# QKV of layer 0 in four K-chunks fed by chunks of modulation products, and four output-projection units in step with attention

## The chip, the cores and the metric

The kernel runs on one NeuronCore of one Trainium2 chip. The metric is the device time of one execution in microseconds (us). Five engines work beside each other, each through its own instructions in order: TensorE (PE: matmuls; PEld: its weight loads), VectorE (DVE), ScalarE (ACT), GpSimd (POOL) and SyncE (SP, which here only issues DMAs). They wait for one another by semaphores.

## The reference

A decoder trunk of two layers on 256 tokens with model width 2048. Each layer is a mixer and a squared-ReLU MLP, both behind an RMS norm with shift and scale from a conditioning vector c, and with a gate on the way back into x. Cut to what the change touches:

```python
cond = silu(c)
for i in range(2):
    mod = cond @ mod_w[i] + mod_b[i]                 # 2048 x (6*2048)
    sh1, sc1, g1, sh2, sc2, g2 = split(mod, 6)
    h = rms_norm(x, norm_mix[i]) * (1 + sc1) + sh1
    y = swa_sink_attention(h, ...) if i == 0 else hgrn2_mixer(h, ...)
    x = x + g1 * y
    h = rms_norm(x, norm_mlp[i]) * (1 + sc2) + sh2
    x = x + g2 * (relu(h @ w1) ** 2 @ w2)

def swa_sink_attention(h, w_in, w_out, q_gain, k_gain, sinks):
    q, k, v = split(h @ w_in, [2048, 2304])          # 32 query heads, 4 kv heads of 64
    q, k = rms_norm(q) * q_gain, rms_norm(k) * k_gain
    # banded blocks of 128 queries against 256 keys, ALiBi, softmax with a sink per head
    return softmax_with_sink(q @ k.T ...) @ v @ w_out
```

All is float32. The change is in layer 0 alone: the modulation products that its norms need, QKV, attention, the output projection and the first quarter of its MLP.

## The kernel before, in words

**Layout.** Activations lie transposed, 16 K-blocks of 128 partitions by 256 tokens. Weights are cut into items of 128 x 2048 floats (1 MB). One table, `seq`, lists all the items of the kernel in one order: weight items ("w") and modulation items. `put` builds it: it lays a stage's weights down and lets modulation items in between them, as its `per` function says. SP issues the loads in this order into five raw buffers (`NRAW`), so a load starts when the item five places ahead of it has been consumed.

**A weight item** (`prep_one`, L237 and L238) is split in two halves: ACT casts a half to a rounded high part `wh`, DVE subtracts to get the low part `wl`. There are buffers for five halves of each (`NW`). A product of float32 accuracy is then three matmuls for each K-block (`three`): wh with the high part of the activation, wh with the low part, wl with the high part. A unit of 128 output columns over 16 K-blocks is 48 matmuls of 256 columns; a weight item always carries 48.

**A modulation item** comes in two kinds. Kind "m" is one column block of 128 outputs: DVE multiplies the transposed weights with the broadcast `cond` and sums (L226, one instruction over 2048 elements and one that reads the accumulator). Kind "g" is a quarter of the K range for four column blocks: PE multiplies four groups of 512 columns in float32 with c as a 32-column weight (`gemv`); four such items make a set, and then ACT copies the row out of PSUM, PE turns it with four transposes (`gt`), and DVE reduces it into `mods`.

**The order of layer 0.** First 16 "m" items (shift and scale 1 of K-blocks 0 to 7), of which `make_h` makes h of the first eight K-blocks. Then QKV: ten items over K-blocks 0 to 7 (`mm_half`), with eight "m" items between them; five over K-blocks 8 to 11 (`mm_quarter`), with eight "m" items; five over K-blocks 12 to 15. The sums of the K-ranges are kept in `parts`: ACT copies the first, DVE adds the second (`add_part`, L798), and the last goes on to the head norms (`done_part`). Behind the last quarter come 24 "g" and four "m" items (gate 1, and scale and shift 2 of the first blocks).

Attention runs in 21 steps (`step`), three after each of the last three QKV items. Step s makes the scores of head pair s (`pair`), turns the probabilities of pair s-3 (`pair_t`), multiplies pair s-4 with v (`pair_v`), and takes up to two modulation items (`GPS`). Once 16 steps are done, two output-projection units start (`mm_std` with `count=2`), and the remaining steps run between their K-blocks. Then `open_mlp` runs the other 14 output units mixed with eight items of the first MLP quarter over K-blocks 0 to 7 (`order`: "o" and "u"), with one modulation item before each, and eight items over K-blocks 8 to 15 ("h", `mm_half`). Each "o" unit ends in a residual update (L568), in `make_u` for the first eight blocks (L553) and in a norm sum (L486). After that come the rest of MLP 0 and layer 1.

**What sets the order of an engine.** The program is written as one list of calls, and a scheduler with a cost model of its own fixes each engine's order before the run. `hook` and `later` place small follow-up work a few slots on. On the chip no engine passes over a waiting instruction.

## Time and profile before

| what | value |
|---|---|
| median of 3 runs | 2331.94 us (2331.55 to 2334.79) |
| profiled execution, its own time | 2334.28 us |
| its span in the trace | 2332.5 us |
| granted TensorE clock, mean | 0.987 |
| PE busy | 2263.7 us, 97% of the span |
| DVE busy | 1818.7 us, 78% |
| ACT busy | 1166.8 us, 50% |
| DMA, mean over the span | 257 GB/s |

The busy share is an average over stages that differ. In the page's 40 slices PE shows "2" in the first and "9" or "8" in all others, so what PE does not use lies almost wholly in the first 60 us; layer 0 up to the end of the opening of its MLP is the first fifth of the span.

### The profile page before, as it was taken

Reading aid. Unit: us, or ns where it says so; the run is one execution under the profiler, and the core shown is the slowest. Engines: PE = TensorE matmul, PEld = TensorE weight load, DVE = VectorE, ACT = ScalarE, POOL = GpSimd, SP = SyncE. Lnnn points to the kernel's source line nnn. Section 1 sums busy time; section 2 is a strip of 40 time slices with the busy share of each in tenths; the row PEclk is TensorE's granted clock in tenths of the full one; section 3 lists DMA queues with packets and bytes.
Section 4 is the critical chain, followed back from the end, with each engine's and each line's share of the span. In section 5 each row is a group of like instructions: output and inputs, shape, how many; then the busy total and the mean of one; then the engine's idle time right before and its main releaser. Section 6 shows DMA issues by size and latency. Waiting matters only on the chain.

```text
span 2332.5 us, 36840 instructions
## 1 busy us (share of the span) xinstructions
PE 2263.7 (97%) x14538; PEld 1986.2 (85%) x14538; DVE 1818.7 (78%) x3061; ACT 1166.8 (50%) x1974; POOL 3.5 (0%) x10
## 2 busy tenths in 40 slices
PE   2989999999999999999999999999999999999999
PEld 0986489998888888888888988899888888888888
DVE  8888788966988988887998988767866766655665
ACT  2435754544444444455666666655544444444443
POOL 0000000000000000000000000000000000000000
PEclk6999999999999999999999999999999999999999
DMA  9987789556989889885577777545666666555552
GB/s 379 344 311 287 295 319 365 200 183 244 341 319 340 319 326 334 322 304 181 210 280 267 257 271 266 201 166 181 226 244 219 249 231 229 209 182 194 184 197 93
DMA packets 84637, 598.79 MB, mean 257 GB/s; under 512 B 9456, under 2 KB 11504, under 8 KB 12272
## 3 DMA queue, kind: packets, MB, share of 16 engines
q1 hardware_dynamic: 81936, 593.81, 70.7%
q8 instruction: 114, 1.87, 0.3%
q10 hardware_dynamic: 2304, 2.10, 0.3%
q0 software_dynamic: 224, 0.52, 0.1%
q14 instruction: 59, 0.48, 0.1%
HBM read 594.04 MB, written 2.10 MB: 256 GB/s over the span
## 4 chain that ended last, share of the span: by engine, by line
PE 94%; DVE 4%; DMA 1%; ACT 1%; issue 1%; ACTq 0%; DVEq 0%
PE mm L50 89%; DVE raw L226 2%; DVE wl L238 1%; PE S L50 1%; PE A L50 1%; PE pv L50 1%; PE pt L50 1%; DMA raw<-in_mod_w_dram 1%; PE on L50 0%; PE cb L50 0%; ACT wh L237 0%; PE ss L50 0%; DVE ht L534 0%; PE ssq L50 0%; PE sst L50 0%
## 5 line engine op out<-in xcount | busy, mean ns | idle before, releaser
L237 ACT CAST wh<-raw 128x1024 fp32r<-128x1024 f32 x744 | 779.3, 1051 | 892.3 <-PE mm L50 801.8
L238 DVE TENSOR_TENSOR wl<-raw,wh 128x1024 fp32r<-128x1024 f32 x744 | 907.3, 1223 | 401.7 <-ACT wh L237 399.3
L50 PE MATMUL mm<-h,wh 128*128 128x512 f32 (+2 forms) x3728 | 1152.6, 368 | 37.3 <-ACT wh L237 37.3
L50 PE MATMUL mm<-h,wl 128*128 128x256 f32 (+1 forms) x3232 | 907.2, 281 | 7.5 <-DVE wl L238 7.5
L50 PE MATMUL mm<-o,wh 128*128 128x512 f32 (+2 forms) x3120 | 859.1, 345 | 0.0
L50 PEld LDWEIGHTS mm<-h,wh 128*128 128x128 f32 x3728 | 672.2, 190 | 162.0 <-ACT wh L237 38.3
L50 PE MATMUL mm<-o,wl 128*128 128x256 f32 (+1 forms) x2432 | 679.5, 280 | 0.0
L50 PEld LDWEIGHTS mm<-h,wl 128*128 128x128 f32 x3232 | 612.4, 190 | 9.5 <-DVE wl L238 8.4
L50 PEld LDWEIGHTS mm<-o,wh 128*128 128x128 f32 x3120 | 538.3, 188 | 81.5 <-issue 1.3
L50 PEld LDWEIGHTS mm<-o,wl 128*128 128x128 f32 x2432 | 458.3, 189 | 0.4
L226 DVE CUSTOM_DVE_ANT_0 raw<-raw,cond 128x2048 f32<-128x2048 f32 x164 | 374.4, 2286 | 15.6 <-DMA raw<-in_mod_w_dram 11.5
L50 PE MATMUL mm<-wh,h 128*128 128x256 f32 x576 | 106.5, 284 | 4.2 <-DVE h L539 2.7
L50 PEld LDWEIGHTS mm<-wh,h 128*128 128x128 f32 x576 | 89.8, 190 | 5.3 <-DVE h L539 3.2
L50 PE MATMUL mm<-wl,h 128*128 128x256 f32 x288 | 81.5, 283 | 0.0
L459 ACT COPY w<-mm 128x256 f32<-128x256 f32 x186 | 67.7, 364 | 0.0
L463 ACT CAST h<-w 128x256 fp32r<-128x256 f32 x125 | 49.9, 404 | 25.6 <-DVE w L919 25.0
L50 PEld LDWEIGHTS mm<-wl,h 128*128 128x128 f32 x288 | 54.7, 190 | 0.6 <-issue 0.4
L919 DVE SCALAR_TENSOR_TENSOR w<-w 128x256 f32<-128x256 f32 x125 | 52.1, 423 | 2.2
L464 DVE TENSOR_TENSOR h<-w,h 128x256 fp32r<-128x256 f32 x125 | 51.7, 419 | 0.0
L460 DVE TENSOR_TENSOR w<-mm,w 128x256 f32<-128x256 f32 x109 | 45.6, 418 | 0.4 <-ACT w L459 0.2
L940 DVE TENSOR_TENSOR acc<-mm,acc 128x256 f32<-128x256 f32 x96 | 40.6, 423 | 6.2 <-PE mm L50 3.7
L939 DVE TENSOR_TENSOR acc<-acc,w 128x256 f32<-128x256 f32 x94 | 39.4, 419 | 7.1 <-ACT w L938 7.0
(200 smaller groups left out, 1098.4 us busy)
## 6 DMA issues: line engine op xcount, KB each, us to landing
raw<-in_mod_w_dram SPq DMA_DIRECT2D x164, 1024.0 KB, 5.7
raw<-in_mlp_dram SPq DMA_DIRECT2D x128, 1024.0 KB, 4.9
raw<-in_hin_dram SPq DMA_DIRECT2D x64, 1024.0 KB, 4.9
raw<-in_mlp1b_dram SPq DMA_DIRECT2D x64, 1024.0 KB, 4.9
raw<-in_mlp1a_dram SPq DMA_DIRECT2D x48, 1024.0 KB, 5.8
raw<-in_mod_g_dram SPq DMA_DIRECT2D x28, 1024.0 KB, 6.6
raw<-in_aout_dram SPq DMA_DIRECT2D x16, 1024.0 KB, 7.0
raw<-in_m1h_dram SPq DMA_DIRECT2D x16, 1024.0 KB, 6.6
```

The costliest lines, as they stand in the source:

```text
L50: r = fn(*args, **kw)
L226: dve.tensor_tensor_reduce(out=r, in0=r, in1=cond, scale=1.0, scalar=0.0, op0=ALU.mult, op1=ALU.add, accum_out=mods[:, e[1], e[2]:e[2] + 1])
L237: act.copy(out=wh, in_=part)
L238: dve.tensor_tensor(out=wl, in0=part, in1=wh.bitcast(F32), op=ALU.subtract)
L459: act.copy(out=t, in_=ps[:, T:])
L460: dve.tensor_tensor(out=out_t, in0=ps[:, :T], in1=t, op=ALU.add)
L463: act.copy(out=opt[:, :T], in_=src_t)
L464: dve.tensor_tensor(out=opt[:, T:2 * T], in0=src_t, in1=opt[:, :T].bitcast(F32), op=ALU.subtract)
L919: dve.scalar_tensor_tensor(out=t, in0=t, scalar=0.0, in1=t, op0=ALU.max, op1=ALU.mult)
L939: dve.tensor_tensor(out=acc[n], in0=acc[n], in1=t, op=ALU.add)
L940: dve.tensor_tensor(out=acc[n], in0=ps[:, :T], in1=acc[n], op=ALU.add)
```

## The change

The table `seq` is rebuilt for layer 0, and the code that walks it with it.

- All of shift 1 is now made by "g" items (four sets), scale 1 by "m" items. QKV runs in four chunks of four K-blocks, each five weight items (`ainq`). The kernel opens with four "g" and four "m" items for chunk 0; chunk 0 to 2 carry, between their weights, the four "g" and four "m" items of the next chunk. `mm_quarter` is called for all four chunks: `first_part` copies, two times `add_part` adds, `done_part` finishes.
- Gate 1 is made wholly by "g" items (16), with four for scale 2 of blocks 0 to 3. These 20 lie between the last weights of chunk 3 and four new items `aoutk`, which hold output units 0 to 3 in K order.
- `wo_step` takes one K-block of the attention output and multiplies it into units 0 to 3 at once (12 matmuls, in two PSUM tiles). From step 9 on, a step runs up to two of them, one step behind `pair_v`, and takes one modulation item.
- The other 12 output units and eight MLP items follow: eight "o", then "o" and "u" in turn, then four "u". Two modulation items go before each of the weights 1 to 6 and 9 to 16, none before the others. Scale and shift 2 of blocks 4 to 15 are all "m" items, those of blocks 0 to 3 "g" items. `make_u` for the eight blocks runs at once, ahead of the ninth weight.
- The PSUM tags `sm` and `pt` (one buffer each) become one tag `sp` with two. The transposes behind a set (`fin`) come two slots later. `ahead` holds modulation items back only where it looks ahead.

In all there are 40 "g" items in place of 28 and 152 "m" items in place of 164. Every item is 1 MB, so the bytes are the same.

```diff
-    seq += two(0, SC1, SH1, 0, KH)
-    put([a["ain"][i] for i in range(10)], two(0, SC1, SH1, KH, 4), per=lambda i: i - 1)
-    put([a["ainq"][0, i] for i in range(5)], two(0, SC1, SH1, KH + 4, 4), per=lambda i: 2 * i)
-    gemvs = gsets([(0, G1, 0), (0, G1, 4), (0, G1, 8), (0, SC2, 0), (0, SH2, 0), (0, SC2, 4), (0, SH2, 4)])
...
-    order = [("o", n) for n in range(8)]
-    late = [("o", n) for n in range(8, 16)]
+    gsh = gsets([(0, SH1, 4 * c) for c in range(4)])
+    gga = gsets([(0, G1, 4 * c) for c in range(4)], 4)
+    gsc, gsf = gsets([(0, SC2, 0)], 8), gsets([(0, SH2, 0)], 9)
+    seq += gsh[:4] + mods_of(0, SC1, 0, 4)
+    for c in range(3):
+        nxt = [e for p in zip(gsh[4 * c + 4:4 * c + 8], mods_of(0, SC1, 4 * c + 4, 4)) for e in p]
+        put([a["ainq"][c, i] for i in range(5)], nxt, per=lambda i: 2 * i)
+    gga += gsc
+    put([a["ainq"][3, i] for i in range(5)] + [a["aoutk"][i] for i in range(4)], gga,
+        per=lambda i: (0, 0, 0, 3, 6, 9, 11, 13, 17)[i])
+    m2 = gsf + two(0, SC2, SH2, 4, 4)
+    order = [("o", n) for n in range(4, 12)]
+    late = [("o", n) for n in range(12, 16)]
     half1 = [("u", n) for n in range(8)]
+    NO = len(order)
     while late:
-        order.append(late.pop(0))
-        if len(late) < 8 - LEAD and half1:
-            order.append(half1.pop(0))
+        order += [late.pop(0), half1.pop(0)]
     order += half1
-    put([a["aout"][n] if k == "o" else a["m1h"][0, n] for k, n in order],
-        gemvs[24:] + two(0, SC2, SH2, KH, KH),
-        per=lambda i: i)
+    put([a["aout"][n - 4] if k == "o" else a["m1h"][0, n] for k, n in order],
+        m2 + two(0, SC2, SH2, KH, KH),
+        per=lambda i: min(len(m2), 2 * i) if i <= NO else len(m2) + 2 * (i - NO))
...
-                tp = psum.tile([P, 4, P], F32, tag="sm", name="gt", bufs=1)
+                tp = psum.tile([P, 4, P], F32, tag="sp", name="gt", bufs=2)
...
-            fin()
+            later(2, fin)
...
+        def wo_step():
+            k = wo["k"]
+            if k == 0:
+                wo["ps"] = [mmtile() for _ in range(2)]
+            if k % 4 == 0:
+                ahead(0)
+                wo["w"] = W.pop(st["w"])
+                st["w"] += 1
+            wh, wl = wo["w"][k % 4 // 2]
+            for u in range(4):
+                c = slice((k % 2 * 4 + u) * P, (k % 2 * 4 + u + 1) * P)
+                three(wo["ps"][u // 2][:, u % 2 * T:(u % 2 + 1) * T], wh[:, c], wl[:, c], O[k],
+                      k == 0 and u % 2 == 0, k == KB - 1 and u % 2 == 1)
+            wo["k"] += 1
...
-            for _ in range(GPS):
-                if seq[st["prep"]][0] != "w":
-                    prep_one()
+            if s_ >= 9:
+                for _ in range(2):
+                    if wo["k"] <= min(KB - 1, s_ - 5):
+                        wo_step()
+            hook()
+            if seq[st["prep"]][0] != "w":
+                prep_one()
+            ahead(0, False)
...
-        for s_, fin_part in enumerate((add_part, done_part)):
-            k0 = KH + 4 * s_
-            feed.need(k0 + 4)
-            if s_ == 1:
-                fill[0], st["hold"] = step, True
-            ahead(LAG - 1)
+        for s_, fin_part in enumerate((first_part, add_part, add_part, done_part)):
+            feed.need(4 * s_ + 4)
+            st["hold"] = s_ == 3
+            ahead(LAG - 1, False)
             for e in range(5):
-                mm_quarter(H, k0, (False, e == 0), (fin_part(2 * e), fin_part(2 * e + 1)))
+                mm_quarter(H, 4 * s_, (False, e == 0), (fin_part(2 * e), fin_part(2 * e + 1)))
...
-        while steps[0] < 16:
+        while wo["k"] < KB:
             step()
         st["hold"] = False
-
...
-        mm_std(O, lambda ps: ev0(next(cnt))(ps), count=2, fold=True)
...
+        for u in range(4):
+            resid(0, G1, u, wo["ps"][u // 2][:, u % 2 * T:(u % 2 + 1) * T])
```

How this moves instructions, at the three places that matter below. First, PE at the very start (`cb` broadcasts c, `ss`, `sst` and `rb` belong to the first norm, `mm<-raw,cst` are the matmuls of "g" items, `mm<-h` those of QKV). Before:

```order
L50 MATMUL cb<-cd,ones 128x512 x4
L50 MATMUL ss<-w,ones 32x256 x16
L50 MATMUL sst<-cst,ssum 128x1 x2
L50 MATMUL rb<-dg,ones 128x256
L50 MATMUL mm<-h_237,wh 128x256 x2
```

and now:

```order
L50 MATMUL cb<-cd,ones 128x512 x4
L50 MATMUL mm<-raw,cst 32x512 x8
L50 MATMUL ss<-w,ones 32x256 x16
L50 MATMUL mm<-raw,cst 32x512
L50 MATMUL sst<-cst,ssum 128x1 x2
L50 MATMUL mm<-raw,cst 32x512 x4
L50 MATMUL rb<-dg,ones 128x256
L50 MATMUL mm<-raw,cst 32x512 x3
L50 MATMUL gt<-cst,w 128x128 x4
L50 MATMUL mm<-raw,cst 32x512 x4
L50 MATMUL mm<-h_264,wh 128x256 x2
```

Five "g" items, the fifth of them for chunk 1, now stand ahead of the first matmul of QKV.

Second, DVE in chunk 1 (the `o_...` rows add a PSUM tile into a part, two for each weight item; `ISA` is an "m" item; `ht` begins h of a later K-block; `wl` is the split of the next weight item). Now:

```order
L810 TENSOR_TENSOR o_340<-mm,o_340 128x512
L227 ISA raw,mods<-raw,cond 128x2048
L227 ISA mods 128x1
L810 TENSOR_TENSOR o_341<-mm,o_341 128x512
L519 TENSOR_TENSOR mods<-mods,cst 128x2
L527 SCALAR_TENSOR_TENSOR gsc<-mods,cst 128x2
L535 SCALAR_TENSOR_TENSOR ht<-x_75,gsc,rbs 128x256 x2
L239 TENSOR_TENSOR wl<-raw,wh 128x1024 x2
L810 TENSOR_TENSOR o_342<-mm,o_342 128x512
```

The split of the third weight item stands behind the add of the second item's last tile (`o_341`) and behind two `ht`. Before, the same stretch of the third quarter held two "m" items and the same adds.

Third, DVE in the output projection after attention (`x` rows are the residual update of a unit, `ssum` its norm sum). Before, with one "m" item to each unit:

```order
L226 ISA raw_3052,mods_81<-raw_3052,cond_72 128x2048
L226 ISA mods_81 128x1
L568 SCALAR_TENSOR_TENSOR x0_73<-mm_3156,mods_81,x0_73 128x256
L238 TENSOR_TENSOR wl_3221<-raw_3042,wh_3220 128x1024
L553 SCALAR_TENSOR_TENSOR h3_3209<-x0_73,gsc_139,h3_3209 128x256
L486 TENSOR_TENSOR ssum_3112<-ssum_3112,w_3251 128x256
L238 TENSOR_TENSOR wl_3287<-raw_3070,wh_3286 128x1024
```

and now, where "o" and "u" alternate:

```order
L227 ISA raw_3378,mods_81<-raw_3378,cond_72 128x2048
L227 ISA mods_81 128x1
L227 ISA raw_3388,mods_81<-raw_3388,cond_72 128x2048
L569 SCALAR_TENSOR_TENSOR x2_75<-mm_3528,mods_81,x2_75 128x256
L487 TENSOR_TENSOR ssum_3255<-ssum_3255,w_3622 128x256
L239 TENSOR_TENSOR wl_3519<-raw_3444,wh_3518 128x1024
L239 TENSOR_TENSOR wl_3523<-raw_3444,wh_3522 128x1024
```

Two "m" items now stand ahead of each weight's split there, which follows the residual of the unit before.

## The prediction

> **What bounds the kernel now.** I read the page first, then the engines' busy time cut into stages, then the waits of PE.

> ```profile
> span 2332.5 us, 36840 instructions
> PE 2263.7 (97%) x14538; PEld 1986.2 (85%) x14538; DVE 1818.7 (78%) x3061; ACT 1166.8 (50%) x1974; POOL 3.5 (0%) x10
> ```

> ```profile
> core 0: us, PE busy (x) PEld busy (x) DVE busy (x) ACT busy (x) POOL busy (x), PEclk, DMA share, GB/s
> 0.00:62.80 62.80, 14.38 (x46) 5.61 (x46) 52.89 (x111) 14.91 (x35) 0.87 (x5) 0.67 0.97 377
> 62.80:163.60 100.80, 93.34 (x721) 92.33 (x722) 87.47 (x102) 41.14 (x51) 0.00 (x0) 0.92 0.91 340
> 163.60:307.50 143.90, 140.57 (x937) 84.15 (x936) 108.49 (x419) 87.40 (x267) 2.07 (x4) 1.00 0.75 282
> 307.50:481.00 173.50, 173.50 (x1459) 173.06 (x1459) 159.83 (x263) 91.25 (x142) 0.00 (x0) 1.00 0.79 286
> ...
> 120.00:160.00 40.00, 33.01 (x244) 32.30 (x243) 39.34 (x50) 13.24 (x17) 0.00 (x0) 0.89 0.92 344
> ```

> ```profile
> PE mm L50 <- ACT wh L237: 37.3, 2, 37.1
> PE mm L50 <- DVE wl L238: 7.5, 4, 2.9
> ```

> PE is the bound from 163.6 us on: in the third and fourth stage it misses 3.3 us and nothing. Of its 68.8 idle us, 48.4 lie ahead of QKV (62.80 less 14.38) and 7.5 in QKV's first three quarters. There DMA (377 GB/s) and DVE set the pace; late in QKV it is DVE (39.34 of 40 us) while PE waits for splits. The stages end at these instructions:

> ```profile
> 62.80 0.79 PE L50 MATMUL mm<-h,wh 128*128 128x256 f32 x2 [37.09 <-ACT wh L237]
> 166.61 0.69 DVE L644 TENSOR_TENSOR o<-mm,o 128x512 f32<-128x512 f32 x1 [1.01 <-PE mm L50]
> 307.53 0.88 DVE L568 SCALAR_TENSOR_TENSOR x<-mm,mods,x 128x256 f32<-128x256 f32 x2 [1.42 <-PE mm L50]
> 479.86 0.88 DVE L900 SCALAR_TENSOR_TENSOR w<-mm,sums,w 128x256 f32<-128x256 f32 x2 [0.38 <-PE mm L50]
> ```

> QKV's first matmul; the evacuation of K, half an item into the last quarter (so that quarter began near 163.6); the residuals of the first two output units; the last of the MLP opening. Between the last two lie 30 weight items (14 "o", 8 "u", 8 "h"): 172.3/30 = 5.74 us of PE for one.

> **The cost of a "g" item and of the steps of DVE.**

> ```profile
> 295.19 1.06 PE L50 MATMUL mm<-raw,cst 128*32 128x512 f32 x8
> 296.19 0.38 PE L50 MATMUL mm<-o,wh 128*128 128x256 f32 x1
> ...
> 236.06 0.60 PE L50 MATMUL gt<-cst,w 128*128 128x128 f32 x4
> 236.59 1.07 PE L50 MATMUL mm<-raw,cst 128*32 128x512 f32 x8
> ```

> From start to start a "g" item is 1.00 us of PE, a set's transposes 0.53. An "m" item is DVE's:

> ```profile
> 134.99 0.68 DVE L798 TENSOR_TENSOR o<-mm,o 128x512 f32<-128x512 f32 x1
> 135.59 0.15 DVE L518 TENSOR_TENSOR mods<-mods,cst 128x2 f32<-128x2 f32 x1
> 135.84 0.88 DVE L534 SCALAR_TENSOR_TENSOR ht<-x,gsc,rbs 128x256 f32<-128x256 f32 x2
> 136.64 2.36 DVE L238 TENSOR_TENSOR wl<-raw,wh 128x1024 fp32r<-128x1024 f32 x2
> 138.91 0.88 DVE L539 SCALAR_TENSOR_TENSOR h<-ht,mods,h 128x256 fp32r<-128x256 f32 x2
> ...
> 319.90 0.48 DVE L568 SCALAR_TENSOR_TENSOR x<-mm,mods,x 128x256 f32<-128x256 f32 x1
> 320.30 1.22 DVE L238 TENSOR_TENSOR wl<-raw,wh 128x1024 fp32r<-128x1024 f32 x1
> 321.43 0.48 DVE L553 SCALAR_TENSOR_TENSOR h<-x,gsc,h 128x256 fp32r<-128x256 f32 x1
> 321.83 0.42 DVE L486 TENSOR_TENSOR ssum<-ssum,w 128x256 f32<-128x256 f32 x1
> 322.16 1.22 DVE L238 TENSOR_TENSOR wl<-raw,wh 128x1024 fp32r<-128x1024 f32 x1
> 323.30 2.29 DVE L226 CUSTOM_DVE_ANT_0 raw<-raw,cond 128x2048 f32<-128x2048 f32 x1
> 325.51 0.09 DVE L226 DVE_READ_ACCUMULATOR2_ANT mods<- 128x1 f32 x1
> ```

> Start to start: add 0.60; bias and gsc 0.25; two `ht` 0.80; a split 2.27 (half of it 1.14); "m" 2.21; residual 0.40, `make_u` 0.40, norm sum 0.33. The last seven rows are one unit of the output projection: 5.6 us of DVE beside 5.74 of PE. It fits by a hair.

> **The change part by part.**

> *Opening and chunk 0.* Ahead of the first weight now lie eight items, not 16. It helps little by itself, since chunk 0 then runs at the DMA's rate: its last weight is item 21, behind 21 x 1.049 + 2.4 (x, constants) = 24.4 MB; at 377 GB/s and some 1.5 us to start, 66.2 us. Cast and half a split, 2.3 us, then 5.74 + 1.0 of PE: chunk 1 starts on PE at 75.2. Chunk 0 has no adds (ACT copies) and its four "g" items are hidden by the DMA.

> *Chunks 1 and 2.* PE has 5 x 5.74 + 4 x 1.00 + 0.53 = 33.2 us of work in each, DMA 13 items, 13.6 MB, 36.2 us at 377. But by the order quoted above the third item's split stands behind the add of the second's last tile, so PE waits: 0.60 + 0.25 + 0.80 + 1.14, less the two matmuls that need no low part (0.24) = 2.55. Behind the third and the fourth item the same without `ht`: 1.50 and 1.75. Together 5.8, so a chunk takes 39.0. DMA fits below that. Chunk 3 starts at 75.2 + 78 = 153.2 in place of 163.6: **-10.4**. Bounds: at the DMA's 36.2 a chunk, -16.0; at the 340 GB/s of the second stage throughout (24.4 MB take 71.8, a chunk 40.1), 1.5 + 71.8 + 9.0 + 80.2 = 162.5, so -1.1. That is also why half the idle time isn't won: the 16 shift items have become PE work (16 x 1.0 + 2.1) inside this stretch.

> *Chunk 3 and attention.* From its start to the last K-block of the output units run in step: eight "g" items and two sets' transposes fewer (-9.1), two output units more (+11.5): **+2.4** on the 143.9. PE was full there, so filling steps with output units moves work and hides none. Bounds: -0.9 if the 3.3 idle us fill up; +7 if a step loses 0.25 us, of 21, to waits that "g" items filled before. DVE has 25% to spare; the four residuals lie beside two "g" items.

> *The rest of the output projection and MLP opening.* Two units fewer (-11.5), four "g" items and a set's transposes (+4.5): **-7.0**.

> *What DVE does to it.* Here the change makes a new wait. Weights 3 to 6 and 9 to 16 now have two "m" items each: DVE per "o" unit 2 x 2.21 + 2.27 + 0.40 + 0.33 = 7.4; per "u" (no residual, small sums) about 7.1. PE has 5.74. "m" items are consumed in order, ahead of the split, and the split stands behind the residual of the unit before, so DVE cannot run far ahead. First stretch: four intervals of 1.7 short, 6.8 (eight `make_u`, 3.2 us, are caught up in the two weights without items). Second: from the first "u" on seven intervals, 1.5 short each, 10.5. The last three "u" and eight "h" have spare DVE time, but what PE has lost by then stays lost: **+17.3**. Bounds: 0 if DVE somehow leads; +26 if the DMA also lags, since three items at 340 GB/s take 9.25 us, 2.0 more than DVE in each of eight intervals, less the lead of five raw buffers (8 us).

> Twelve "m" items fewer on DVE in all (26.5 us) lie in QKV and attention, beside PE, and are worth what is counted there. The merged PSUM tags: the page shows waits of PE for them of 0.9 us (pt) and less; nothing. After 481 us nothing is moved.

> **The sum.** -10.4 + 2.4 - 7.0 + 17.3 = +2.3. The profiled execution took 2334.3 (span and 1.8 around it), so 2336.6; the median of the runs is 2.3 below that execution, hence 2334.3. Forecast: **2334 us, no change**. This kernel's measurement can tell 0.2%, 4.7 us: faster is below 2327, slower above 2337.

> [...] Whether the many short waits slow the clock matters:

> ```profile
> 137.91 0.58 PE L50 MATMUL mm<-h,wl 128*128 128x256 f32 x1 [2.76 <-DVE wl L238]
> 138.29 0.63 PE L50 MATMUL mm<-h,wh 128*128 128x256 f32 x2
> ...
> 146.73 0.38 PE L50 MATMUL mm<-h,wl 128*128 128x256 f32 x1 [1.29 <-DVE wl L238]
> 146.95 0.40 PE L50 MATMUL mm<-h,wh 128*128 128x256 f32 x2
> ```

> Behind a wait of 2.76 us two matmuls span 0.63 us, behind one of 1.29 they span 0.40 (the granted clock of that stretch was 0.89). The new waits of 1.5 to 2.55 lie between. I add nothing. [...]

> **The rivals.**

> *PE runs through the output projection.* DVE gets its "m" items done early, or the first stretch's slack carries on. For it: DVE has 25% spare in attention. Against: the table holds those items back until attention is over. Without the +17.3: 2317. Chance 0.17.

> *The chunks run at the DMA's rate.* The waits for adds vanish because the next "g" falls into them. For it: "g" items stand near those places. Against: by the order PE meets them twelve matmuls into the item, behind the wait. Chunk 3 at 147.6: 5.6 less, 2329. Chance 0.10.

> *Slower: the clock drops at the waits.* In the doubled stretches PE waits once in each item, 11 times, for about 1.5 us. If each halves the clock, four to nine groups of three matmuls at 0.64 in place of 0.355 follow: 1.1 to 2.5 us each, so 12 to 27; at the middle 2353. It decides from the length at which a wait counts: below 1.5 us all do, above 2.6 none. Against it stands the row at 146.73. Chance 0.12.

> *Slower: the DMA lags DVE there.* The bound of +26: 2343. For it: 340 GB/s in QKV; against: 377 in the opening. Chance 0.12.

> *The opening brings nothing,* chunk 3 near 162.5: 2344. Chance 0.07.

> **How the numbers follow.** The forecast has 0.42, with a range of its own of 2326 to 2342 (a part of it lies beyond each bound). Faster: 0.17, half of the second rival and 0.05 of the forecast, 0.27. Slower: 0.12 + 0.12 + 0.07 and 0.03 of the forecast, 0.34. Same: 0.39. The range reaches to the first rival less some luck in the opening and into the third: 2316 to 2349.

> **What would show it.** First QKV matmul near 37 us; the evacuation of K of chunk 3 (L647) near 156; waits of PE for `wl` of 1.5 to 2.6 us, three to a chunk; the four residuals near 300 (153 + 146); then DVE at 95% or more with waits of PE for `wl` of 1 to 2 us, 17 us in all, up to the fourth "u"; the last of the opening near 482. If PE shows no waits after attention, the first rival holds and the residuals' place alone decides. I'm wrong altogether if attention itself takes 10 us more or less than 146.

## The result and the profile after

| what | before | after |
|---|---|---|
| median of 4 runs | 2332.27 us (2331.55 to 2334.79) | 2366.8 us (2366.19 to 2367.27) |
| profiled execution, its own time | 2334.28 us | 2367.27 us |

The ratio is 1.0146, with a 95% interval of 1.0128 to 1.0164: the change makes the kernel 1.5% slower, by some 34 us. The forecast of 2334 us, its range up to 2349 included, is wrong.

First the head of the page of the changed kernel:

```profile
span 2365.5 us, 37076 instructions
PE 2295.2 (97%) x14646; PEld 2005.8 (85%) x14646; DVE 1799.9 (76%) x3050; ACT 1163.8 (49%) x1977; POOL 3.5 (0%) x10
```

PE is "97% busy" as before and yet 31.5 us busier, with 108 matmuls more out of 14,646: most of the lost time counts as busy. Then the four instructions at which the stages end, from the timeline (start, duration, engine, line):

```profile
41.13 0.80 PE L50 MATMUL mm<-h,wh 128*128 128x256 f32 x2 [5.04 <-ACT wh L238]
...
173.90 0.68 DVE L647 TENSOR_TENSOR o<-mm,o 128x512 f32<-128x512 f32 x1
...
304.07 1.27 DVE L569 SCALAR_TENSOR_TENSOR x<-mm,mods,x 128x256 f32<-128x256 f32 x3 [2.67 <-PE mm L50]
...
513.90 0.88 DVE L911 SCALAR_TENSOR_TENSOR w<-mm,sums,w 128x256 f32<-128x256 f32 x2 [0.60 <-PE mm L50]
```

Beside the four rows of before:

| stretch | before | after | difference | forecast |
|---|---|---|---|---|
| start to K of the last quarter | 166.6 | 173.9 | +7.3 | -10.4 |
| from there to the first residuals | 140.9 | 130.2 | -10.7 | +2.4 |
| from there to the end of the MLP opening | 172.3 | 209.8 | +37.5 | +10.3 |
| the rest | 1852.6 | 1851.6 | -1.0 | 0 |

All three terms of the forecast missed, two upwards and one downwards. The engines' busy time of the changed kernel in stages (us of the stage; then for each engine its busy us and instructions; the granted clock, the DMA engines' busy share and GB/s). The first row ends at the first QKV matmul, the next three are chunks 0 to 2, then chunk 3 with attention, 16 units behind it, and the last 12:

```profile
0.00:41.13 41.13, 19.67 (x90) 6.51 (x91) 22.55 (x74) 13.74 (x32) 0.87 (x5) 0.87 0.95 379
41.13:86.30 45.17, 38.52 (x277) 33.06 (x278) 28.19 (x36) 19.07 (x27) 0.00 (x0) 0.93 0.85 322
86.30:128.30 42.00, 36.54 (x278) 30.77 (x279) 29.37 (x43) 12.58 (x16) 0.00 (x0) 0.96 0.91 324
128.30:170.90 42.60, 37.16 (x275) 32.35 (x274) 29.99 (x43) 13.46 (x18) 0.00 (x0) 0.92 0.90 319
170.90:304.00 133.10, 132.91 (x949) 91.40 (x949) 104.41 (x412) 87.02 (x267) 2.07 (x4) 1.00 0.63 225
304.00:440.00 136.00, 114.77 (x813) 107.60 (x812) 106.76 (x149) 42.04 (x71) 0.00 (x0) 0.89 0.88 332
440.00:514.00 74.00, 72.09 (x588) 71.43 (x587) 68.47 (x128) 43.70 (x69) 0.00 (x0) 0.98 0.61 210
```

The row from 304 to 440 us holds most of the loss behind attention. It has 16 weight items and a set of "g" items, by the forecast's prices 16 x 5.74 + 4.5 = 96.3 us of PE. It takes 136.0: 21.2 us PE is idle, and for 114.8 it is busy, 18.5 more than the work costs at the full clock. The granted clock there was 0.89; 0.11 of 136 us are 15.0, so the clock accounts for at most some 15 of the 18.5, and the other 3 to 4 stay open. DVE is busy for 106.8 us of 136, 78%. So DVE's throughput, on which the forecast's +17.3 rests, is not what fills this stretch. The waits of PE in it (in all, times, the longest):

```profile
PE mm L50 <- ACT wh L238: 15.0, 11, 2.1
PE mm L50 <- DVE wl L239: 4.7, 7, 0.8
PE sst L50 <- DVE ssum L487: 1.5, 1, 1.5
```

PE waits above all for ACT's casts (`wh`), and ACT is busy for 42 us of these 136. An engine with two thirds of its time free is late: that points to order, not to work. Here is one such place in the timeline, between an "o" unit and the "u" item behind it; rows of PE, DVE, ACT and of SP's issue of the load:

```profile
389.30 0.28 PE L50 MATMUL mm<-o,wl 128*128 128x256 f32 x1
391.60 0.51 PE L50 MATMUL mm<-h,wh 128*128 128x258 f32 x2 [2.02 <-ACT wh L238]
392.55 0.80 PE L50 MATMUL mm<-h,wh 128*128 128x258 f32 x2 [0.44 <-ACT wh L238]
393.14 0.42 PE L50 MATMUL mm<-h,wl 128*128 128x258 f32 x1
393.36 0.63 PE L50 MATMUL mm<-h,wh 128*128 128x258 f32 x2
...
389.62 0.48 DVE L569 SCALAR_TENSOR_TENSOR x<-mm,mods,x 128x256 f32<-128x256 f32 x1 [0.24 <-PE mm L50]
390.64 0.42 DVE L487 TENSOR_TENSOR ssum<-ssum,w 128x256 f32<-128x256 f32 x1 [0.54 <-ACT w L486]
391.58 2.36 DVE L239 TENSOR_TENSOR wl<-raw,wh 128x1024 fp32r<-128x1024 f32 x2 [0.51 <-ACT wh L238]
...
390.20 0.42 ACT L486 ACTIVATE w<-x 128x256 f32<-128x256 f32 x1 [6.42 <-DVE x L569]
390.52 1.98 ACT L238 CAST wh<-raw 128x1024 fp32r<-128x1024 f32 x2
...
377.96 0.33 SPq L213 DMA_DIRECT2D raw<-in_m1h_dram  x1
```

Read from top to bottom by start: PE ends the unit at 389.58; DVE makes its residual (389.62); ACT, which had stood idle for 6.42 us behind that residual, squares it (390.20) and only then casts the next weight (390.52), a weight whose load SP had issued at 377.96; PE starts at 391.60, waits for the second half's cast, and then runs its matmuls at 0.63 us a pair in place of 0.40. The cast of a weight begins only when the unit before has ended, and until its first half is done PE has no matmul to run.

DVE's order in the trace shows how often this happens. Behind attention there are 12 residuals of single units; at 6 of them (units 7 to 9 and 13 to 15) the next weight is not yet split when the residual runs. In chunks 1 and 2 the split of the next weight stands behind the add at 14 of 20 adds.

### The profile page after: what moved, and what is told of

It reads as the page before. It is cut to its first block, busy times and chain, and to the rows that moved or that the text cites. A ratio compares the mean times of both kernels' runs of the same rounds, so it can differ in the third digit from the quotient of the medians.

```text
span 2365.5 us, 37076 instructions
## 1 busy us (share of the span) xinstructions
PE 2295.2 (97%) x14646; PEld 2005.8 (85%) x14646; DVE 1799.9 (76%) x3050; ACT 1163.8 (49%) x1977; POOL 3.5 (0%) x10
## 4 chain that ended last, share of the span: by engine, by line
PE 94%; DVE 4%; ACT 1%; issue 1%; DMA 0%; ACTq 0%; DVEq 0%
PE mm L50 89%; DVE raw L227 2%; DVE wl L239 1%; ACT wh L238 1%; PE S L50 1%; PE A L50 1%; PE pt L50 1%; PE pv L50 1%; PE on L50 0%; PE cb L50 0%; DVE o L810 0%; PE ss L50 0%; PE sst L50 0%; DVE x L569 0%; PE ot L50 0%
## 5 line engine op out<-in xcount | busy, mean ns | idle before, releaser
L238 ACT CAST wh<-raw 128x1024 fp32r<-128x1024 f32 x744 | 777.4, 1050 | 880.4 <-PE mm L50 767.8
L50 PE MATMUL mm<-h,wh 128*128 128x512 f32 (+2 forms) x3728 | 1163.7, 370 | 20.1 <-ACT wh L238 17.2
L50 PE MATMUL mm<-h,wl 128*128 128x256 f32 (+1 forms) x3232 | 910.5, 283 | 8.9 <-DVE wl L239 8.9
L50 PE MATMUL mm<-o,wh 128*128 128x512 f32 (+2 forms) x3120 | 870.2, 349 | 9.7 <-ACT wh L238 9.7
L50 PEld LDWEIGHTS mm<-h,wh 128*128 128x128 f32 x3728 | 676.2, 191 | 159.2 <-ACT wh L238 21.9
L50 PE MATMUL mm<-o,wl 128*128 128x256 f32 (+1 forms) x2432 | 684.3, 282 | 4.3 <-DVE wl L239 4.3
L50 PEld LDWEIGHTS mm<-o,wh 128*128 128x128 f32 x3120 | 546.3, 191 | 96.5 <-ACT wh L238 11.8
L50 PEld LDWEIGHTS mm<-h,wl 128*128 128x128 f32 x3232 | 614.5, 190 | 12.1 <-DVE wl L239 10.6
L50 PEld LDWEIGHTS mm<-o,wl 128*128 128x128 f32 x2432 | 461.5, 190 | 6.6 <-DVE wl L239 5.6
L227 DVE CUSTOM_DVE_ANT_0 raw<-raw,cond 128x2048 f32<-128x2048 f32 x152 | 346.8, 2285 | 14.0 <-DMA raw<-in_mod_w_dram 14.0
L50 PE MATMUL mm<-wh,h 128*128 128x256 f32 x576 | 107.5, 286 | 3.3 <-DVE h L540 2.2
L50 PEld LDWEIGHTS mm<-wh,h 128*128 128x128 f32 x576 | 90.4, 191 | 5.1 <-DVE h L540 2.9
L50 PE MATMUL mm<-wl,h 128*128 128x256 f32 x288 | 81.7, 284 | 0.0
L50 PE MATMUL mm<-raw,cst 128*32 128x512 f32 x320 | 49.3, 637 | 7.8 <-DMA raw<-in_mod_g_dram 7.8
L50 PEld LDWEIGHTS mm<-wl,h 128*128 128x128 f32 x288 | 55.1, 191 | 0.2
L486 ACT ACTIVATE w<-x 128x256 f32<-128x256 f32 x45 | 18.1, 406 | 58.8 <-DVE x L569 58.0
```

Source lines behind the costliest of these rows:

```text
L50: r = fn(*args, **kw)
L227: dve.tensor_tensor_reduce(out=r, in0=r, in1=cond, scale=1.0, scalar=0.0, op0=ALU.mult, op1=ALU.add, accum_out=mods[:, e[1], e[2]:e[2] + 1])
L238: act.copy(out=wh, in_=part)
L486: act.activation(out=sq, in_=X[kb], func=AF.Square)
```

## The experiments

The theories from here on: **1, order** (as just read: the split and the cast of the next weight stand behind the end of the item before); **2, DVE's throughput** (the forecast); **3, the loads**. The 44.5 us of the first expectation are 209.8 less 165.3, the price of that part without any wait (172.3 - 7.0).

### pin: only the order, behind attention

A dependency without a semaphore puts one instruction behind another on its own engine; all work and all loads stay.

```diff
+    def behind(r, w, split):
+        if st["pin"] and w in made:       # made[w]: last cast and last split of weight w
+            tc.add_manual_dep(r.ins, made[w][split], NoSync, reason="issue order")
...
-        dve.scalar_tensor_tensor(out=X[n], ...)
+        r = dve.scalar_tensor_tensor(out=X[n], ...)
+        behind(r, st["w"] + 1, 1)
```

and so for the norm's square (`made[w][0]`), the sums and the copies of a "u" item.

> Same table, same products, same bytes as the change; only the order on DVE and ACT differs: behind attention, the residual and the norm square of an output unit (and the sums and copies of an MLP unit) now stand behind the cast and the split of the next weight item, where in the changed kernel they stand ahead of them in the two doubled stretches. Behind attention the changed kernel takes 209.8 us, 44.5 more than the 165.3 that the units, g items and spare work need. Theory 1 (order: cast, split and the unit's matmuls run one after the other, because the cast waits for the residual of the unit before): the doubled intervals fall from 9 to 11.5 us to what DVE needs, 7.1 to 7.4, so the 44.5 fall to some 17 and the time from 2366.8 to about 2340. Theory 2 (DVE throughput, as forecast): the loss is DVE's already, no gain, 2360 to 2367. Theory 3 (DMA: three items at 340 GB/s take 9.25 us to each doubled interval): at most 8 us are won, 2358 to 2367.

Measured: 2345.8 us, ratio 1.0058 (1.0043 to 1.0073) against the kernel before; 21 us less than the change. The part behind attention takes 187.2 us. Theory 1 said 2340, theories 2 and 3 at least 2358: the order makes up half of the 44.5 us (22.6). The same place now, from the timeline of DVE, and the stretch behind attention in two windows:

```profile
340.38 2.35 DVE L248 TENSOR_TENSOR wl<-raw,wh 128x1024 fp32r<-128x1024 f32 x2
342.65 0.47 DVE L580 SCALAR_TENSOR_TENSOR x<-mm,mods,x 128x256 f32<-128x256 f32 x1
343.05 2.28 DVE L236 CUSTOM_DVE_ANT_0 raw<-raw,cond 128x2048 f32<-128x2048 f32 x1
...
305.00:440.00 135.00, 121.83 (x958) 116.21 (x958) 123.92 (x185) 56.91 (x95) 0.00 (x0) 0.96 0.96 379
440.00:492.30 52.30, 52.30 (x442) 52.26 (x442) 49.05 (x92) 29.00 (x46) 0.00 (x0) 1.00 0.53 182
```

The split stands ahead of the residual, PE does 958 instructions in 135 us in place of 813 in 136, and the DMA engines now move 379 GB/s with a share of 0.96, where they moved 332 in the changed kernel. Some 22 us of the 44.5 are still there, and DMA is nearly full: theory 3 is the next to be tried.

### pin_nodma and pin_short: what is left, loads or DVE

```diff
+            if e[0] != "m" or e not in spare:
                 sp.dma_start(out=r, ...)
...
-            dve.tensor_tensor_reduce(out=r, in0=r, in1=cond, ...)
+            dve.tensor_tensor_reduce(out=r, in0=cond if e in spare else r, in1=cond, ...)
```

> As the run with the new order, and the 24 products of scale and shift 2 of K-blocks 4 to 15 multiply the broadcast c with itself in place of their weights, so their 24 loads of 1 MB fall away (these modulation values are left out of the computation). DVE does the same instructions. If DMA holds the doubled stretches once the order is mended (theory 3), this run is 10 to 25 us faster than the one with the loads; if DVE holds them (theory 2, or theory 1 with DVE as the next bound), the two are within 5 us of each other, near 2340.

Measured: 2334.3 us, ratio 1.0009 (0.9999 to 1.0018), 11.5 less than `pin`; 176.2 us behind attention.

```profile
304.60:440.00 135.40, 128.15 (x1053) 122.98 (x1053) 131.64 (x203) 65.06 (x106) 0.00 (x0) 1.00 0.59 208
440.00:481.00 41.00, 41.00 (x348) 40.96 (x348) 39.21 (x74) 22.41 (x34) 0.00 (x0) 1.00 0.53 180
```

`pin_short` shortens the same 24 products on DVE and keeps their loads:

```diff
+            n = 2 * T if e in spare else D
-            dve.tensor_tensor_reduce(out=r, in0=r, in1=cond, ...)
+            dve.tensor_tensor_reduce(out=r[:, :n], in0=r[:, :n], in1=cond[:, :n], ...)
```

> As the run with the new order, with all loads, but the same 24 products go over 512 of their 2048 elements alone (three quarters of those sums are left out): 24 x 1.65 = 40 us less of DVE. If DVE is the bound behind the order (the forecast's 17 us), nearly all of it goes: 2322 to 2327. If DMA is the bound there, no change against the run with whole products (within 4 us).

Measured: 2341.7 us, ratio 1.0042 (1.0027 to 1.0057), 4 less than `pin`, with 40 us less of DVE's work. So with the order mended the loads cost about 11 us and DVE's work at most about 4, a difference that lies within the two intervals. One reserve on the 11: without those loads the casts also ran further ahead (two to two and a half weights ahead of most residuals, in place of one to two), so a part of them may be order again. With neither loads nor a bad order, DVE is busy 131.6 of 135.4 us: only there does it become the bound that the forecast took it for.

### even_table: the scheduler's own order under another table

```diff
+    gga += gsc + gsf
...
-        per=lambda i: (0, 0, 0, 3, 6, 9, 11, 13, 17)[i])
+        per=lambda i: (0, 0, 0, 3, 6, 9, 12, 16, 21)[i])
-    m2 = gsf + two(0, SC2, SH2, 4, 4)
+    m2 = two(0, SC2, SH2, 4, 4)
...
+        per=lambda i: min(len(m2), i) if i <= NO else len(m2) + -(-4 * (i - NO) // 3))
```

> The change with another table alone: the four g items of shift 2 go into attention, and behind it one modulation item goes before each of the weights 1 to 8 and 4/3 on average before each of the other 12, in place of two in bursts. No order is forced, but the scheduler now puts cast and split of the next weight ahead of the residual for all units except the last. Theory 1: the doubled stretches go, 5 to 10 of the 44.5 us stay, and attention grows by the 4.0 us of the four g items that the later part loses: 2322 to 2332. Theory 3: the 44 items behind attention take 44 x 1.049 MB / 340 GB/s = 136 us beside 115 of PE, so 20 us stay: 2342. Theory 2: DVE has 24 x 2.21 + 20 x 2.27 + 12 x 0.73 = 107 us there, less than PE's 115, so as theory 1.

Measured: 2343.3 us, ratio 1.0046 (1.0029 to 1.0063); 182.8 us behind attention. Theory 3's number (2342) was hit, not theory 1's 2322 to 2332. An even table alone brings nearly what the forced order brings, because with it the scheduler itself put splits ahead at most residuals; the loads then set the rest.

### tags_back: the merged PSUM tags

```diff
-                tp = psum.tile([P, 4, P], F32, tag="sp", name="gt", bufs=2)
+                tp = psum.tile([P, 4, P], F32, tag="sm", name="gt", bufs=1)
```

and so for the other eight tiles of the tag.

> The change with one part undone: the PSUM tag sp with two buffers is again sm and pt with one buffer each. The forecast gave the merge nothing. From the start of chunk 3 to the residuals behind attention the change takes 133.2 us, the kernel before 143.9, though two units more lie there. If the merge did part of that (from start to start the rows of S, pt, pv, sst and gt lie 9 us shorter together), this run is 5 to 9 us slower than the change, 2372 to 2376, and the residuals come 5 to 9 us later. If the g items alone did it (eight fewer, 1.33 us from start to start before), it stays within 2 us of 2366.8.

Measured: 2373.5 us, ratio 1.0175 (1.0158 to 1.0192), 0.0029 or some 7 us more than the change (the two intervals just overlap, at 1.0158 to 1.0164). From K of the last quarter to the residuals, this run and then the change (windows):

```profile
173.40:309.00 135.60, 135.48 (x924) 88.79 (x923) 100.93 (x410) 87.12 (x267) 2.06 (x4) 1.00 0.60 215
...
173.90:304.00 130.10, 129.91 (x924) 88.40 (x923) 101.41 (x409) 86.21 (x266) 2.07 (x4) 1.00 0.62 223
```

The same 924 matmuls take 5.5 us longer with PE "busy" throughout (135.48 of 135.60 us). So what the second buffer saves does not show as idle time of PE (0.12 and 0.19 us), and no row shows where in the busy time it lies.

### open_nodma and open6: the chunks

```diff
+    spare = set(mods_of(0, SC1, 4, 12))      # as in pin_nodma, but scale 1 of K-blocks 4 to 15
```

> The change, with the 12 m items of scale 1 of K-blocks 4 to 15 multiplying the broadcast c with itself, without their loads (these modulation values are left out). DVE, ACT and PE do the same. The chunks of QKV lie 45, 42 and 42.6 us apart on PE; the forecast had 39.0, from 33.2 of PE and three waits for splits. If the loads set the pace (weights land late: ACT waits 26.6 us for four of them between 40 and 175 us), the three chunks fall to 34 to 37 each and the time by 15 to 20, to 2347 to 2352. If the waits for splits behind the adds do, the chunks come down no further than 39: 2356 to 2359. If neither, 2367.

Measured: 2341.2 us, ratio 1.0035 (1.0021 to 1.0048). K of the last quarter comes at 147.1 in place of 173.9. It looks like the loads, and more than expected. But the order had moved too: without those loads the split stands one to two items ahead at all adds.

```diff
+            if st["load"] < PEND and st["load"] % 6 == 5:
+                r = extra.tile([P, D], F32, tag="raw", name="raw")
+            else:
                 r = wpool.tile([P, D], F32, tag="raw", name="raw", bufs=NRAW)
```

> The change with one raw buffer more from the start to the end of attention: six loads ahead in place of five, the same bytes. If the chunks are late because a load starts only when the item five places ahead is consumed, though the DMA engines have time to spare (share 0.87 to 0.90 there, 313 to 335 GB/s, against 399 GB/s at 304 to 324 us), the chunks lose 2 to 4 us each: 2355 to 2361. If the rate of the DMA engines itself holds them, no change: 2365 to 2368.

Measured: 2370.1 us, ratio 1.0157 (1.0142 to 1.0172): no gain. Weights landed sooner (a median of 5.2 us from issue in place of 7.1), and DVE's order of splits and adds was the same as in the change. These two runs alone would have said "the rate of the DMA engines". The next run shows that this would have been wrong.

### open_pin: only the order, in the chunks

```diff
-                dve.tensor_tensor(out=parts[p], in0=ps, in1=parts[p], op=ALU.add)
+                r = dve.tensor_tensor(out=parts[p], in0=ps, in1=parts[p], op=ALU.add)
+                behind(r, st["w"] + 1, 1)
```

> The change with the order of DVE and ACT changed in the first three chunks alone: the copy or the add of each QKV tile now stands behind the cast and the split of the next weight item, where in the changed kernel nearly all adds of chunks 1 and 2 stand ahead of that split. Same table, same loads, same products. Chunks 1 and 2 lie 42.0 and 42.6 us apart there. If the order holds them (as behind attention: a split that waits for the end of the item before), they fall to 35.5 (as in the run without the loads of scale 1) to 38, and with chunk 0 the time by 10 to 20 us: 2347 to 2357. If the 13 loads of a chunk hold them, 13.6 MB at the 320 GB/s of that stretch, nothing changes: 2363 to 2369, and the gain of the run without those loads was DMA's.

Measured: 2341.7 us, ratio 1.0034 (1.0022 to 1.0045), 25 us less than the change, with all loads. Chunks 1 and 2 in its windows, which answer to the third and fourth row of the changed kernel's:

```profile
78.60:114.40 35.80, 35.02 (x287) 30.92 (x288) 29.94 (x42) 13.52 (x17) 0.00 (x0) 1.00 0.99 397
114.40:146.90 32.50, 31.75 (x262) 28.61 (x261) 28.41 (x42) 12.08 (x16) 0.00 (x0) 1.00 1.00 400
```

35.8 and 32.5 us in place of 42.0 and 42.6, at 397 and 400 GB/s in place of 324 and 319, and the clock at 1.00. The loads of the changed kernel were slow because the items ahead of them were consumed late, not the other way round. In chunk 0 of the changed kernel PE had waited for the cast in three of the five items, like this:

```profile
58.99 0.51 PE L50 MATMUL mm<-h,wh 128*128 128x256 f32 x2 [1.62 <-ACT wh L238]
59.94 0.51 PE L50 MATMUL mm<-h,wh 128*128 128x256 f32 x2 [0.44 <-ACT wh L238]
```

### spread, spread_open, orders and before_pin

`spread` is `pin` with another table: 12 of the items behind attention go into it.

```diff
-    gga += gsc
+    m2 = two(0, SC2, SH2, 4, 4)
+    gga = mix(gga + gsc + gsf, m2)           # one m item behind every third g item
...
+            for _ in range(2):
                 if seq[st["prep"]][0] != "w":
                     prep_one()
...
+        per=lambda i: -(-4 * i // 5))
```

> The order of the run 'pin' and another table: the four g items of shift 2 and eight of the 24 m items behind attention go into attention (a step takes up to two items), the other 16 lie evenly, 0.8 to a weight. Behind attention that leaves 36 items, 37.7 MB: 111 us at 340 GB/s, beside 115 of PE, and DVE has 16 x 2.21 + 20 x 2.27 + 12 x 0.73 = 90. If DMA is what the pinned order still waits for (theory 3), the 187.2 us behind attention fall to 161 to 168; attention grows by 4.5 for the g items and 0 to 6 for the m items: 2326 to 2337. If what is left there is neither DMA nor DVE, the part only loses the 4.5 that attention gains: 2345.

Measured: 2334.3 us, ratio 1.0007 (0.9998 to 1.0016). Behind attention 159.8 us: all of the loss there is gone. But the residuals come at 321.4 in place of 304.1. Of these 17.3 us, 2 to 4 are matmuls of the next unit that now lie ahead of them, 4.5 were expected for the "g" items, and 9 to 11 are left over. They are put down to the eight "m" items inside attention, for which at most 6 were allowed; no run shows this by itself.

`spread_open` has this table and both orders, those of `pin` and of `open_pin`; no other line differs.

> The run 'spread' (order and table behind attention mended) with the order of 'open_pin' in the chunks. The parts lie one behind the other, so the gains should add: 2334.3 less what 'open_pin' wins against 2366.8. With the order as the cause in the chunks: 2316 to 2325, faster than the kernel before by 8 to 17 us. With the loads as the cause: 2331 to 2337, no difference from the kernel before.

Measured: 2306.9 us, ratio 0.9882 (0.9866 to 0.9899), 27 us faster than the kernel before. It is the fastest of all the runs, and it leaves nothing of the computation out. Behind attention, in two windows:

```profile
294.80:400.00 105.20, 104.99 (x880) 104.73 (x879) 97.43 (x149) 50.11 (x76) 0.00 (x0) 1.00 0.91 335
400.00:454.80 54.80, 54.80 (x460) 54.62 (x459) 53.60 (x102) 32.89 (x51) 0.00 (x0) 1.00 0.58 207
```

160.0 us, of which PE misses 0.2. The 28 weight items at 5.74 make 160.7: with up to 4 us of a unit begun before them, the forecast's price of this part was right within 4 us, and only the wait was not.

`orders` is the change with its own table and the `behind` lines of `pin` and `open_pin`.

> The changed kernel with its own table and both orders mended ('open_pin' in the chunks, 'pin' behind attention), nothing else. If each is a cause of its own, the gains add: 25.1 us (2366.8 to 2341.7) and 21.0 (2366.8 to 2345.8), so 2320.7, faster than the kernel before by some 13 us, and 14 slower than the run 'spread_open', which has less to load behind attention. If an earlier end of the chunks only moves the loads closer together, up to 8 us of it come back behind attention: 2321 to 2329.

Measured: 2321.3 us, ratio 0.9952 (0.9938 to 0.9967). The gains add: 2320.7 was said, and the interval is some 3 us to either side. So the change as it is written, with its instructions in another order, beats the kernel before by 0.5%.

`before_pin` puts the same lines into the kernel before, for its third quarter and its output projection:

```diff
             k0 = KH + 4 * s_
             feed.need(k0 + 4)
+            st["pin"] = s_ == 0
```

> The kernel before, with the same order given to it: the adds of its third quarter, and the residuals, norm squares, sums and copies of its output projection, behind the cast and the split of the next weight item. If the order alone were a gain whatever the table, this would be faster too. But PE waits there for splits only 7.5 us in all, and not at all behind attention, where halves are split one ahead of use: at most 6 us, 2326 to 2334. If what lies behind the split there (residual, make_u, norm sum) comes late for the next step, it is slower, 2334 to 2340.

Measured: 2330.9 us, ratio 0.9991 (0.9982 to 1.0001): hardly a difference. PE's waits for splits before attention stay as they were (7.9 us in place of 7.5); the forced order did not remove them. It is no gain by itself; in these runs it is worth something only where splits had fallen behind the end of the item before.

## Why the prediction was wrong

**The opening.** The first QKV matmul came at 41.1, not near 37. Rows of DVE, ACT and PE at the start (timeline):

```profile
26.42 0.17 DVE L261 TENSOR_REDUCE mods<-gt 128x4 f32<-128x16 f32 x1 [3.13 <-PE gt L50]
...
26.78 2.28 DVE L227 CUSTOM_DVE_ANT_0 raw<-raw,cond 128x2048 f32<-128x2048 f32 x1
...
39.23 0.91 ACT L539 ACTIVATE h<-ht,mods 128x256 fp32r<-128x256 f32 x2 [5.61 <-DVE ht L535]
40.05 1.98 ACT L238 CAST wh<-raw 128x1024 fp32r<-128x1024 f32 x2
...
34.16 1.94 PE L50 MATMUL mm<-raw,cst 128*32 128x512 f32 x8 [7.78 <-DMA raw<-in_mod_g_dram]
```

The first "m" item stands behind the reduce of the first set, which waits 3.13 us for PE's transposes; from 26.4 us on DVE works nearly without a gap through the four "m" items and the steps of h, ACT finishes h behind it (39.23) and only then casts the first weight (40.05), for which QKV's first matmul waits. The raw buffer of that first "m" item comes free at 29 only, so the "g" item of the next chunk lands late and PE waits 7.78 us for it; that wait is over at 34.2 and does not set the 41.1. No run tests the opening by itself. The larger miss lies in the chunks. "Chunk 0 then runs at the DMA's rate" comes true only once the order is mended: 45.2 us at 322 GB/s in place of 38.2 (75.2 less 37), and 37.0 at 390 GB/s in `spread_open` (41.9 to 78.9), which has the order of `open_pin` in the chunks. For chunks 1 and 2 the mechanism was seen, "the third item's split stands behind the add", and PE's idle time was near the 5.8 us forecast (42.00 - 36.54 = 5.5). What was missing is the clock at these waits: that they cost none ("I add nothing"), no run shows. The granted clock was 0.96 and 0.92, which is up to 1.7 and 3.4 us of the 3.0 and 3.6 by which the chunks are late (42.0 and 42.6 in place of 39.0). PE was busy for 36.5 and 37.2 us with 278 and 275 matmuls, where `open_pin` does 287 and 262 in 35.0 and 31.8. So the step that failed behind "-10.4" is that chunk 0 was given no waits for casts (7.0 us over its 38.2) and the waits of chunks 1 and 2 no loss of clock; chunk 3 begins at 170.9 in place of 153.2, and the term came out as +7.3. With the order mended it starts at 146.9, just before the forecast's best bound (163.6 - 16.0 = 147.6).

**Attention.** The forecast of +2.4 missed by 13 us to the good side, in three of its terms. The groups of PE's instructions in the stretch, the "g" items of before and then of after:

```profile
L50 PE MATMUL mm<-raw,cst 128*32 128x512 f32 x224 | 38.1, 601 | 0.0
...
L50 PE MATMUL mm<-raw,cst 128*32 128x512 f32 x160 | 24.9, 602 | 0.0
```

Eight items fewer (eight matmuls are one) took 13.2 us of busy time with them, not 8.0: a price of 1.00 from one place was taken for 28 that were 1.36 on average. This price is argued from busy time alone, and a run speaks against it: `even_table` has four "g" items and their transposes more inside attention, and its stretch from K of the last quarter to the residuals (173.3 to 308.2) is only 4.7 us longer, near the 4.5 of the forecast's price; at 1.36 each it would be 6.0. The merged tags, set at "nothing" because PE's waits for them were 0.9 us, were worth 5 to 7 us (`tags_back`). And PE's idle time in the stage fell from 3.3 us (143.90 less 140.57) to 0.2 (133.10 less 132.91), which the forecast had only as its bound of -0.9. How the 13 us divide among the three stays open.

**Behind attention.** -7.0 was right: `spread_open` shows 160.0 for work priced at 160.7. The step that failed most is "+17.3" in "What DVE does to it". The forecast quoted the order in which "the split stands behind the residual of the unit before" and concluded that DVE "cannot run far ahead"; then it added up DVE's work for an interval, 7.4 us, and set that against PE's 5.74. It should have followed the chain instead: the unit's end, residual, square, cast, split, the next unit. No matmul lies beside that chain, so an interval is not the larger of DVE and PE but PE's unit plus the way round, about 2.5 us of idle time (2.02 + 0.44 at 391.60), plus what the clock loses. With one or two stretches of 3.41 us at half the clock (see the last section) that is 5.74 + 2.46 + 1.7 or 3.4, an estimate of 9.9 to 11.6 us; the residuals of units 8 and 9 come 11.5 and 10.5 us behind those before them. Measured: +44.5 in place of +17.3; `pin` takes half of it away without touching any work, and of the rest the loads hold about 11 us.

**The rivals.** "The clock drops at the waits", at 12 to 27 us and a chance of 0.12, was no rival but a part of what happened: up to some 15 us in the row from 304 to 440, together with 21.2 of waits, where the forecast had put one in place of the other. "The DMA lags DVE" holds only once the order is mended (11 us, `pin_nodma`). "PE runs through" needed both the order and fewer loads. "The opening brings nothing" was right in its direction, and the 162.5 it gave was still too early.

**What would show it.** Of the signs named, DVE at 95% failed most plainly (78%), and the waits were for `wh` and not for `wl`. In that list stood "wrong altogether if attention takes 10 us more or less": it took 13 less than its 146, and the time still came out slower, because the other two stretches lost 45 us (7.3 and 37.5).

## What to carry to other kernels

Where an engine's order is fixed ahead, a stage's interval is not the sum of the busiest engine's work but the longest chain from one item's end to the next item's start (here 11.5 us at unit 8, in which DVE was busy for 7.7): write that chain down from the built order before adding up any engine, and ask whether the preparation of the next item stands ahead of or behind the end of this one. When idle or slow resources (ACT here busy for 42 of 136 us behind attention, DMA at 319 to 324 GB/s in the chunks, where `open_pin` moved 397 to 400) lie beside a waiting PE, force the order first and look at the rates afterwards; a run that takes work away can move the order too, and then proves less than it seems to.

## What the hardware showed that was not expected

In the changed kernel the granted clock fell behind waits shorter than the 2.76 us of the prediction's row at 137.91, and not always at the same length. A single wait of 1.66 us left it at 1.00; behind waits of 1.60 and 0.76 us close together it was 0.50:

```profile
121.60 0.39 PE L50 MATMUL mm<-h,wl 128*128 128x256 f32 x1 [1.66 <-DVE wl L239]
...
401.46 0.50 PE L50 MATMUL mm<-o,wh 128*128 128x256 f32 x2 [1.60 <-ACT wh L238]
402.72 0.52 PE L50 MATMUL mm<-o,wl 128*128 128x256 f32 x1 [0.76 <-DVE wl L239]
```

```profile
119.50:122.91 3.41, 1.75 (x15) 1.55 (x14) 3.41 (x8) 2.61 (x4) 0.00 (x0) 1.00 1.01 360
122.91:126.33 3.42, 3.42 (x32) 3.42 (x31) 3.42 (x6) 0.69 (x2) 0.00 (x0) 1.00 0.93 323
...
389.16:392.57 3.41, 0.95 (x7) 0.53 (x5) 2.12 (x5) 2.30 (x3) 0.00 (x0) 1.00 0.89 322
392.57:395.98 3.41, 3.41 (x16) 3.41 (x17) 3.41 (x3) 0.00 (x0) 0.00 (x0) 0.50 0.96 334
...
399.40:402.81 3.41, 1.05 (x7) 0.65 (x6) 2.09 (x6) 2.26 (x3) 0.00 (x0) 1.00 0.89 296
402.81:406.22 3.41, 3.41 (x16) 3.41 (x17) 3.41 (x4) 0.00 (x0) 0.00 (x0) 0.50 0.78 245
```

With PE busy for 1.75 of 3.41 us the clock in the next window is 1.00; with 0.95 and 1.05 it is 0.50. Divided in this way, the changed kernel's trace has twelve windows at the full clock between its first QKV matmul and its last matmul in which PE is busy for 0.28 to 0.47 of the window: a window at half the clock follows each of them, and none follows a full-clock window at 0.51 or more. In the trace of the kernel before there are three of them, at 0.26 to 0.46, and none follows one at 0.52 or more. So in these two traces the idle share of a full-clock window tells the two cases apart, and the length of a single wait does not.

The DMA engines moved 397 to 400 GB/s at a share of 0.99 to 1.00 through two whole chunks of `open_pin`. The forecast had reckoned with 377 and, as its bound, with the 340 GB/s of the kernel before; here they moved more beside a PE that was busy for 35.0 of 35.8 and 31.8 of 32.5 us. How much of the 340 was the order of the kernel before, no run shows.
